# A modulation vector computed by rows on VectorE instead of by columns with TensorE sums, and in another stage of the first layer

## The chip, the cores and the metric

The kernel runs on one core of one Trainium2 chip. The metric is the device time of one execution in microseconds (us); lower is better. Several executions are timed, and their median counts.

## The reference

Two trunk layers work on 256 context tokens and 1024 latent tokens of width 1024. Each layer has a mixing part (four groups of recurrent heads: HGRN2, mLSTM, retention and GLA, each scanned forward and backward) and a channel part (a squared-ReLU MLP of width 4096). Ahead of each part the tokens are normalised, scaled and shifted, and behind it a gate scales what is added to the residual. These shifts, scales and gates are the modulation: for each layer a vector of 6 x 1024 numbers for the latent tokens and one for the context tokens.

```python
for layer in range(DEPTH):
    mod_l = (jax.nn.silu(c) @ w_ada[layer] + b_ada[layer])[:, None, :]
    mod_c = (jax.nn.silu(c_ctx) @ w_ada[layer] + b_ada[layer])[None, None, :]
    sh1_l, sc1_l, g1_l, sh2_l, sc2_l, g2_l = jnp.split(mod_l, 6, axis=-1)
    sh1_c, sc1_c, g1_c, sh2_c, sc2_c, g2_c = jnp.split(mod_c, 6, axis=-1)
    pl = split_proj(modulate(xl, sh1_l, sc1_l) @ w_in[layer])
    pc = split_proj(modulate(xc, sh1_c, sc1_c) @ w_in[layer])
    ...
    xl = xl + g1_l * mixer_out(raw_l, pl, g_heads[layer], w_out[layer])
    ...
    xl = xl + g2_l * sq_relu_mlp(modulate(xl, sh2_l, sc2_l), w_ff1[layer], w_ff2[layer])
```

The change is in how `silu(c) @ w_ada + b_ada` is computed, a product of one vector of 1024 with a 1024 x 6144 matrix, for two vectors and two layers.

## The kernel before

Tokens lie along the free dimension, channels on the 128 partitions. Each dense product is made of three matrix products of split operands (`mm3`, lines 293 to 295: high by high, high by low, low by high), so TensorE has most of the work.

The stages of a layer, in order: `mix_open` (normalisation and the first dense products), `mixers`, `outproj`, and `mlp`. In `mixers` the four recurrent groups run one after the other: GLA, HGRN2 (two halves), mLSTM (two halves), retention (two halves). Beside each, `Fill` advances a queue of dense products in small steps, to give TensorE work while the scan waits for VectorE and ScalarE. In the first layer's `mixers` three of five of these steps also advance a generator, `fill.also`, which computes two thirds of layer 0's modulation (r = 1 and 2; the third r = 0 is made at the start, by `ada_unit`). In the first layer's `mlp` the function `filler` advances another such generator behind each of 32 tiles; it computes all of layer 1's modulation. A framework then sets the final order on each engine from this program; the engines work in order, each through its own queue.

The generator is `ada_part`. For each strip of W columns of `w_ada` it loads eight blocks of 128 input rows (128 x W, through SyncE's queue, line 402), and for each token VectorE multiplies a block by the 128 scalars of the vector on the partitions and adds it to an accumulator (lines 406 and 408). Then TensorE sums the accumulator over the partitions by products with a column of ones (line 413), and VectorE adds the bias (line 419). In the first layer W is 256, with four buffers for blocks; in `mlp` W is 512, with four too.

Names: `ph`, `px`, `pw`, `po`, `pc` are SBUF pools of the stages, `st` the pool that stays (constants, temporaries, `mod`), `psum` the PSUM banks. `mod` holds the modulation, 48 columns for each layer and token.

Of the kernel before, what the change touches and what calls it, by code (L numbers as in the profile page):

```python
# [6 lines left out]
F32 = mybir.dt.float32  # L7
# [3 lines left out]
ALU = mybir.AluOpType  # L11
# [4 lines left out]
NK = 8  # L16
# [181 lines left out]
class K:  # L198
    def __init__(self, ctx, tc, io):
# [3 lines left out]
        dp = ctx.enter_context(tc.tile_pool(name="dp", bufs=1, space=bass.MemoryType.DRAM))  # L203
# [12 lines left out]
        self.d_a = dp.tile([2, 4, NC], F32, name="d_a")  # L216

# [98 lines left out]
    def params(self, tmp):  # L316
        nc = self.nc
        c2 = self.o["cc"](256)
        a, b = tmp.sub(0, 256)(256), tmp.sub(256, 256)(256)
        self.logsig(b, c2, a)  # L320
        nc.scalar.activation(b, b, AF.Exp)
        nc.vector.tensor_tensor(c2, c2, b, op=ALU.mult)

# [67 lines left out]
    def ada_part(self, l, r, toks, wring, tmp, acc, banks, W):  # L391


        nc = self.nc
        one = self.m64[:, 1:2]
        nt, nb = len(toks), W // 128
        for q in range(2048 // W):
            g, h = divmod(q * W, 512)
            A = [b(W) for b in acc[:nt]]
            for k in range(NK):  # L400
                w = wring.next()(W)
                nc.sync.dma_start(w, self.io["w_ada"][l, r, k, :, g, h:h + W])
                for i, j in enumerate(toks):
                    c = self.cc[:, k, j:j + 1]
                    if k == 0:
                        nc.vector.tensor_scalar(A[i], w, c, None, op0=ALU.mult)
                    else:
                        nc.vector.scalar_tensor_tensor(A[i], w, c, A[i], op0=ALU.mult, op1=ALU.add)
                yield
            ps = self.bank(banks().next())  # L410
            for i in range(nt):
                for cb in range(nb):
                    nc.tensor.matmul(ps[:, 2 * cb + i:2 * cb + i + 1], lhsT=A[i][:, 128 * cb:128 * cb + 128], rhs=one,  # L413
                                     start=True, stop=True)
            o = 16 * r + nb * q
            mo = self.mod[:, l, o:o + nb, toks[0]:toks[0] + nt]
            bb = self.bada[:, l, o:o + nb].unsqueeze(2).to_broadcast([128, nb, nt])
            v = ps[:, 0:2 * nb].rearrange("p (c j) -> p c j", j=2)[:, :, 0:nt]
            nc.vector.tensor_tensor(mo, v, bb, op=ALU.add)
            if (r == 0 and g >= 2) or (r == 2 and g < 2):  # L420
                nc.vector.tensor_scalar(mo, mo, 1.0, None, op0=ALU.add)
            yield
# [997 lines left out]
    def mixers(self, l, ada):  # L1420
        nc, hp = self.nc, self.heap

        fill = Fill(5)
# [32 lines left out]
        ao = hp.alloc(1536, True) if l == 0 else None  # L1456
        if l == 0:
            fill.also = ada([ao.sub(256 * i, 256) for i in range(6)], lambda: self.dbanks)
# [17 lines left out]
        self.rt_setup()  # L1476
        for p in range(2):
# [93 lines left out]
def build(ctx, tc, io):  # L1571
# [17 lines left out]
    for l in range(2):  # L1589
# [4 lines left out]
        def ada(bufs, banks):  # L1594
            for r in (1, 2):
                yield from b.ada_part(0, r, (0, 1), Ring(bufs[:4]), None, bufs[4:6], banks, 256)
# [8 lines left out]
        def ada1(bufs, l=l):  # L1605
            for r in range(3) if l == 0 else ():
                yield from b.ada_part(1, r, (0, 1) if r == 0 else (1,), Ring(bufs[:4]), None, bufs[4:6], lambda: b.banks, 512)
# [3 lines left out]
        def filler():  # L1611
            for _ in range(4):
                next(gen, None)
# [64 lines left out]
def host(x, c, ctx, c_ctx, w_ada, b_ada, w_in, g_heads, hgrn_lb_logits, ml_gate_bias, rt_decay_logit,  # L1678
# [29 lines left out]
    A["w_ada"] = ca(w_ada.reshape(2, 8, 128, 3, 4, 512).transpose(0, 3, 1, 2, 4, 5))  # L1708
# [29 lines left out]
```

## Time and profile before

| | us |
|---|---|
| median of 3 runs | 3308.24 |
| lowest, highest | 3303.61, 3309.18 |
| the profiled execution, its own time | 3300.05 |
| its span, first to last instruction | 3298.2 |
| TensorE busy | 3215.6 (97%) |
| VectorE busy | 2121.8 (64%) |
| ScalarE busy | 1286.1 (39%) |
| TensorE's granted clock, mean | 0.992 of full speed |

An engine's busy time says little where matrix products are pipelined; what ends last is read from the chain, the sequence of steps followed back from the last instruction, and from who waited for whom in a stretch. In the rows, PE is TensorE, PEld its weight load, DVE VectorE, ACT ScalarE, POOL GpSimd, and SP SyncE, whose queue (SPq) issues the transfers.

### The profile page before, as it was taken

Reading aid. Unit: us, or ns where it says so; the run is one execution under the profiler, and the core shown is the slowest. Engines: PE = TensorE matmul, PEld = TensorE weight load, DVE = VectorE, ACT = ScalarE, POOL = GpSimd, SP = SyncE. Lnnn points to the kernel's source line nnn. Section 1 sums busy time; section 2 is a strip of 40 time slices with the busy share of each in tenths; the row PEclk is TensorE's granted clock in tenths of the full one; section 3 lists DMA queues with packets and bytes.
Section 4 is the critical chain, followed back from the end, with each engine's and each line's share of the span. In section 5 each row is a group of like instructions: output and inputs, shape, how many; then the busy total and the mean of one; then the engine's idle time right before and its main releaser. Section 6 shows DMA issues by size and latency. Waiting matters only on the chain.

```text
span 3298.2 us, 52930 instructions
## 1 busy us (share of the span) xinstructions
PE 3215.6 (97%) x20936; PEld 2640.0 (80%) x20936; DVE 2121.8 (64%) x4218; ACT 1286.1 (39%) x2665; POOL 10.8 (0%) x41
## 2 busy tenths in 40 slices
PE   7998899999999999999999999999999999999998
PEld 4786688877888888888888678788778888888887
DVE  4778887787666656555655586866756555554546
ACT  4665565445322122121212565765445322222222
POOL 0000000000000000000000000000000000000000
PEclk9999899999999999999999999999999999999999
DMA  5113444434322222222211222333315111111111
GB/s 206 61 50 127 122 133 148 121 101 146 103 80 71 83 65 80 69 64 64 77 39 34 76 66 77 110 114 109 103 58 163 53 50 46 51 51 46 51 48 65
DMA packets 175010, 278.85 MB, mean 85 GB/s; under 512 B 21097, under 2 KB 66825, under 8 KB 174505
## 3 DMA queue, kind: packets, MB, share of 16 engines
q1 hardware_dynamic: 173464, 273.66, 26.5%
q8 instruction: 164, 2.69, 0.3%
q10 hardware_dynamic: 1296, 1.81, 0.2%
q14 instruction: 86, 0.70, 0.1%
HBM read 229.75 MB, written 45.64 MB: 83 GB/s over the span
## 4 chain that ended last, share of the span: by engine, by line
PE 88%; DVE 5%; DMA 3%; ACT 3%; issue 1%; SPq 0%; DVEq 0%; ACTq 0%
PE psum L293 23%; PE psum L294 23%; PE psum L295 23%; PE psum L830 2%; PE psum L600 2%; PE psum L631 2%; PE psum L633 2%; PE psum L632 1%; PE psum L817 1%; PE psum L833 1%; PE psum L1018 1%; PE psum L705 1%; PE psum L1357 1%; PE psum L413 1%; DVE px L990 1%
## 5 line engine op out<-in xcount | busy, mean ns | idle before, releaser
L525 DVE SCALAR_TENSOR_TENSOR x<-psum,st,x 128x512 f32<-128x512 f32 (+1 forms) x648 | 441.3, 690 | 213.2 <-PE psum L295 212.3
L281 ACT ACTIVATE pc<-st 128x512 fp32r<-128x512 f32 x256 | 161.2, 632 | 847.5 <-PE psum L294 808.7
L294 PE MATMUL psum<-pc,pc 128*128 128x512 f32 (+1 forms) x1296 | 475.9, 367 | 0.0
L293 PE MATMUL psum<-pc,pc 128*128 128x512 f32 (+1 forms) x1296 | 475.8, 367 | 0.0
L295 PE MATMUL psum<-pc,pc 128*128 128x512 f32 (+1 forms) x1296 | 473.8, 366 | 0.0
L293 PE MATMUL psum<-Hhi,pc 128*128 128x512 f32 (+1 forms) x1280 | 471.9, 369 | 1.7 <-ACT pc L281 1.5
L294 PE MATMUL psum<-Hlo,pc 128*128 128x512 f32 (+1 forms) x1280 | 471.9, 369 | 0.1
L295 PE MATMUL psum<-Hhi,pc 128*128 128x512 f32 (+1 forms) x1280 | 470.5, 368 | 0.0
L293 PE MATMUL psum<-Hhi,pw 128*128 128x512 f32 (+1 forms) x1192 | 451.0, 379 | 5.7 <-ACT pw L281 2.5
L295 PE MATMUL psum<-Hhi,pw 128*128 128x512 f32 (+1 forms) x1192 | 445.2, 374 | 0.0
L294 PE MATMUL psum<-Hlo,pw 128*128 128x512 f32 (+1 forms) x1192 | 444.8, 373 | 0.0
L504 DVE TENSOR_TENSOR st<-st 128x256 f32<-128x256 f32 (+1 forms) x160 | 101.8, 637 | 301.8 <-ACT pc L503 300.7
L293 PEld LDWEIGHTS psum<-pc,pc 128*128 128x128 f32 x1296 | 244.4, 189 | 43.8 <-DVE x L525 1.3
L295 PEld LDWEIGHTS psum<-pc,pc 128*128 128x128 f32 x1296 | 244.0, 188 | 43.0 <-issue 2.7
L294 PEld LDWEIGHTS psum<-pc,pc 128*128 128x128 f32 x1296 | 244.5, 189 | 41.3 <-issue 2.1
L293 PEld LDWEIGHTS psum<-Hhi,pc 128*128 128x128 f32 x1280 | 241.2, 189 | 43.5 <-ACT pc L281 2.4
L294 PEld LDWEIGHTS psum<-Hlo,pc 128*128 128x128 f32 x1280 | 241.3, 189 | 40.9 <-DVE Hlo L481 0.5
L295 PEld LDWEIGHTS psum<-Hhi,pc 128*128 128x128 f32 x1280 | 241.1, 188 | 40.9 <-DVE pc L282 0.6
L293 PEld LDWEIGHTS psum<-Hhi,pw 128*128 128x128 f32 x1192 | 226.7, 190 | 51.4 <-issue 10.1
L282 DVE TENSOR_TENSOR pc<-st,pc 128x512 fp32r<-128x512 f32 x256 | 175.5, 690 | 137.9 <-ACT pc L281 117.3
L295 PEld LDWEIGHTS psum<-Hhi,pw 128*128 128x128 f32 x1192 | 226.2, 190 | 37.6 <-issue 2.1
L294 PEld LDWEIGHTS psum<-Hlo,pw 128*128 128x128 f32 x1192 | 226.8, 190 | 36.2 <-issue 2.2
(398 smaller groups left out, 4950.4 us busy)
## 6 DMA issues: line engine op xcount, KB each, us to landing
st<-w_ff SPq DMA_DIRECT2D x256, 256.0 KB
st<-w_inT SPq DMA_DIRECT2D x96, 256.0 KB
ph<-w_ada SPq DMA_DIRECT2D x128, 128.0 KB
st<-w_out SPq DMA_DIRECT2D x50, 256.0 KB
pc<-w_ada SPq DMA_DIRECT2D x48, 256.0 KB
st<-w_ada SPq DMA_DIRECT2D x48, 256.0 KB
d_z<-st SPq DMA_DIRECT2D x40, 256.0 KB
ps<-w_ada SPq DMA_DIRECT2D x32, 256.0 KB
```

The costliest lines, as they stand in the source:

```text
L281: nc.scalar.activation(hi, raw, AF.Copy)
L282: (eng or nc.vector).tensor_tensor(lo, raw, F(hi), op=ALU.subtract)
L293: t.matmul(out, lhsT=w[0], rhs=m[0], start=first, stop=False)
L294: t.matmul(out, lhsT=w[0], rhs=m[1], start=False, stop=False)
L295: t.matmul(out, lhsT=w[1], rhs=m[0], start=False, stop=last)
L413: nc.tensor.matmul(ps[:, 2 * cb + i:2 * cb + i + 1], lhsT=A[i][:, 128 * cb:128 * cb + 128], rhs=one, start=True, stop=True)
L504: nc.vector.tensor_tensor(r, r, r, op=ALU.mult)
L525: nc.vector.scalar_tensor_tensor(x, ps, self.mod[:, l, 40 + o, j:j + 1], x, op0=ALU.mult, op1=ALU.add)
L600: t.matmul(ps[:, 0:304], lhsT=h[a], rhs=u[b], start=(k + i == 0), stop=(k == NK - 1 and i == 2))
L631: t.matmul(ps[:, e, :], lhsT=h[0], rhs=u[0], start=(k == 0), stop=False)
L633: t.matmul(ps[:, e, :], lhsT=h[1], rhs=u[0], start=False, stop=(k == NK - 1))
L830: nc.tensor.matmul(o, lhsT=ST[r0:r0 + kd, c, d, :], rhs=qd[d](c)[r0:r0 + kd, :], start=(j == 0), stop=False, tile_position=(r0, 0))
```

## The change

`ada_part` is replaced by `ada_rows`. The weights are stored transposed, so that an output column lies on a partition and the 1024 inputs along the row. For each token and each half of 512 inputs, the vector is loaded once, copied to all 128 partitions (from `d_c` in DRAM, to which GpSimd's queue writes it at the start). Then for each of 16 blocks of 128 outputs, 512 weights for each output are loaded, and one VectorE instruction multiplies them by the copied vector and writes the sum along the row to a scratch column in the other layer's part of `mod`. TensorE has no part in it. The weights are loaded once for each token, not once for both.

In the first layer the generator starts later: not ahead of HGRN2, but ahead of mLSTM. It has two buffers of 128 x 512 for weights and one for the vector, in place of four of 128 x 256 and two accumulators, and its transfers are issued from GpSimd's queue. In `mlp` there are four buffers for weights and two for the vector, on SyncE's queue, and `filler` takes three steps instead of four.

```diff
+            nc.gpsimd.dma_start(self.d_c[j].rearrange("(k p) -> p k", p=128), self.cc[:, :, j])
...
-    def ada_part(self, l, r, toks, wring, tmp, acc, banks, W):
...
-            for k in range(NK):
-                w = wring.next()(W)
-                nc.sync.dma_start(w, self.io["w_ada"][l, r, k, :, g, h:h + W])
-                for i, j in enumerate(toks):
-                    c = self.cc[:, k, j:j + 1]
-                    if k == 0:
-                        nc.vector.tensor_scalar(A[i], w, c, None, op0=ALU.mult)
-                    else:
-                        nc.vector.scalar_tensor_tensor(A[i], w, c, A[i], op0=ALU.mult, op1=ALU.add)
-                yield
-            ps = self.bank(banks().next())
-            for i in range(nt):
-                for cb in range(nb):
-                    nc.tensor.matmul(ps[:, 2 * cb + i:2 * cb + i + 1], lhsT=A[i][:, 128 * cb:128 * cb + 128], rhs=one,
-                                     start=True, stop=True)
...
+    def ada_rows(self, l, r, toks, wring, cs, queue):
...
+        S = self.mod[:, 1 - l, 0:16, :]
+        for j in toks:
+            for h in range(2):
+                c = cs.next()(512)
+                queue.dma_start(c, self.d_c[j:j + 1, 512 * h:512 * h + 512].to_broadcast([128, 512]))
+                for o in range(16):
+                    w = wring.next()(512)
+                    queue.dma_start(w, self.io["w_adaT"][l, r, o, :, 512 * h:512 * h + 512])
+                    nc.vector.scalar_tensor_tensor(w, w, 1.0, c, op0=ALU.mult, op1=ALU.mult,
+                                                   accum_out=S[:, o:o + 1, h])
+                    if o % 2:
+                        yield
+            mo = self.mod[:, l, 16 * r:16 * r + 16, j]
+            nc.vector.tensor_tensor(mo, S[:, :, 0], S[:, :, 1], op=ALU.add)
+            nc.vector.tensor_tensor(mo, mo, self.bada[:, l, 16 * r:16 * r + 16], op=ALU.add)
...
-            fill.also = ada([ao.sub(256 * i, 256) for i in range(6)], lambda: self.dbanks)
...
+        ao = hp.alloc(1536, True) if l == 0 else None
+        if l == 0:
+            fill.also = ada([ao.sub(512 * i, 512) for i in range(3)])
...
-                yield from b.ada_part(0, r, (0, 1), Ring(bufs[:4]), None, bufs[4:6], banks, 256)
+                yield from b.ada_rows(0, r, (0, 1), Ring(bufs[:2]), Ring(bufs[2:]), nc.gpsimd)
...
-                yield from b.ada_part(1, r, (0, 1) if r == 0 else (1,), Ring(bufs[:4]), None, bufs[4:6], lambda: b.banks, 512)
+                yield from b.ada_rows(1, r, (0, 1) if r == 0 else (1,), Ring(bufs[:4]), Ring(bufs[4:]), nc.sync)
...
-            for _ in range(4):
+            for _ in range(3):
```

Three places show what moves. The first is VectorE's queue in the first layer, at the start of mLSTM's first half (`px` and `ph` hold the scan's operands). Before, the modulation has no instruction in this piece:

```order
L1338 TENSOR_TENSOR px_0_688<-px_0_688,psum 128x384
L1351 TENSOR_TENSOR px_0_688<-psum,st 128x390 x2
L1338 TENSOR_TENSOR px_0_688<-px_0_688,psum 128x384
L1360 TENSOR_TENSOR px_0_688<-px_0_688,psum 128x390
L1334 TENSOR_TENSOR ph_0_251<-ph_0_251,st 128x384
L1334 TENSOR_TENSOR px_0_688<-px_0_688,st 128x384
L1360 TENSOR_TENSOR px_0_688<-px_0_688,psum 128x390
```

With the change, the same scan instructions (their lines are six lower) have pairs of the row product (line 406) between them:

```order
L406 SCALAR_TENSOR_TENSOR ph_0_254,st<-ph_0_254 128x512 x2
L1332 TENSOR_TENSOR px_0_691<-px_0_691,psum 128x384 x3
L1345 TENSOR_TENSOR px_0_691<-psum,st 128x390 x2
L1354 TENSOR_TENSOR px_0_691<-px_0_691,psum 128x390 x2
L406 SCALAR_TENSOR_TENSOR ph_0_254,st<-ph_0_254 128x512
L1360 TENSOR_TENSOR px_0_691<-px_0_691,st 128x12
L406 SCALAR_TENSOR_TENSOR ph_0_254,st<-ph_0_254 128x512
L1361 RECIPROCAL px_0_691<-px_0_691 128x12
```

So two row products stand behind every few scan instructions, 128 in all from the head of mLSTM to the last gates of `mixers`; the 160 products of the old form ahead of mLSTM are gone from VectorE's queue.

The second is GpSimd's queue, which held no transfer before. From the head of mLSTM it holds (`MEMSET` of `px` are the scan's state columns):

```order
L402 DMA ph_0_254<-d_c 128x512
L1283 MEMSET px_0_691 128x65
L405 DMA ph_0_254<-w_adaT 128x512 x2
L1284 MEMSET px_0_691 128x65
L405 DMA ph_0_254<-w_adaT 128x512 x15
L402 DMA ph_0_254<-d_c 128x512
L405 DMA ph_0_254<-w_adaT 128x512 x10
```

All 128 loads of weights and 8 of the vector stand there, one behind the other; each waits for the row product that last read its buffer, two products back.

The third is VectorE's queue in the first layer's `mlp`, at its second tile (line 498 squares an activation, line 499 makes its low part, line 283 the low part of a weight tile):

```order
L406 SCALAR_TENSOR_TENSOR pc_4_8587,st<-pc_4_8587,st 128x512
L406 SCALAR_TENSOR_TENSOR pc_5_8588,st<-pc_5_8588,st 128x512
L498 TENSOR_TENSOR st<-st 128x256
L406 SCALAR_TENSOR_TENSOR st<-st 128x512
L499 TENSOR_TENSOR pc_9_8592<-st,pc_8_8591 128x256
L406 SCALAR_TENSOR_TENSOR st<-st 128x512
L498 TENSOR_TENSOR st<-st 128x512
L406 SCALAR_TENSOR_TENSOR pc_4_8587,st<-pc_4_8587,st 128x512
L499 TENSOR_TENSOR pc_9_8592<-st,pc_8_8591 128x512
L406 SCALAR_TENSOR_TENSOR pc_5_8588,st<-pc_5_8588,st 128x512
L406 SCALAR_TENSOR_TENSOR st<-st 128x512 x2
L283 TENSOR_TENSOR pc_0_8583<-st,pc_0_8583 128x512
```

Here the 128 products of the second layer stand from the second to the 20th of the 96 low parts (line 499) of the stage. The 128 of the old form stood from ahead of the first to behind the 76th.

## Rows read from the trace of the kernel before

**Rows 1.** The page: busy time (share of the span) and number of instructions.

```profile
PE 3215.6 (97%) x20936; PEld 2640.0 (80%) x20936; DVE 2121.8 (64%) x4218; ACT 1286.1 (39%) x2665; POOL 10.8 (0%) x41
```

**Rows 2.** The page: the chain that ended last, by engine.

```profile
PE 88%; DVE 5%; DMA 3%; ACT 3%; issue 1%; SPq 0%; DVEq 0%; ACTq 0%
```

**Rows 3.** Windows: length, busy us of each engine (instructions), clock, DMA share, GB/s.

```profile
200.00:553.00 353.00, 324.98 (x3418) 264.75 (x3398) 290.12 (x734) 204.68 (x465) 1.28 (x12) 0.96 0.38 118
553.00:817.00 264.00, 260.81 (x1809) 211.95 (x1807) 200.89 (x508) 126.55 (x320) 0.24 (x2) 1.00 0.40 119
...
952.00:1120.00 168.00, 168.00 (x887) 144.78 (x885) 110.95 (x181) 34.62 (x62) 0.00 (x0) 1.00 0.25 74
```

**Rows 4.** Windows of line 413 alone: PE, PEld busy us.

```profile
200.00:553.00 353.00, 10.43 (x72) 10.60 (x72) 0.96 0.38 118
553.00:817.00 264.00, 6.95 (x56) 7.33 (x56) 1.00 0.40 119
```

**Rows 5.** The chain from 937 to 1810 us, by line.

```profile
by line: PE psum L293 32.6%; PE psum L294 32.5%; PE psum L295 32.3%; PE psum L413 1.5%; DMA pc<-w_ada 0.5%; DVE st L476 0.5%; DVE Hlo L481 0.3%; DVE st L408 0.2%; DVE st L406 0.0%; issue 0.0%; DVEq L408 0.0%
```

**Rows 6.** Windows of line 408 alone: DVE busy us.

```profile
200.00:553.00 353.00, 62.57 (x140) 0.96 0.38 118
553.00:817.00 264.00, 37.18 (x84) 1.00 0.40 119
952.00:1120.00 168.00, 28.20 (x40) 1.00 0.25 74
```

**Rows 7.** Waits of PE, 200 to 553 us: total, times, longest.

```profile
PE psum L1018 <- DVE px L990: 10.3, 6, 4.6
PE psum L833 <- ACT px L1043: 6.2, 5, 3.0
PE psum L413 <- DVE ph L408: 3.5, 1, 3.5
```

**Rows 8.** Waits of PE, 553 to 817 us: all there are.

```profile
PE psum L1343 <- DVE px L802: 0.8, 1, 0.8
PE psum L1329 <- DVE px L1351: 0.6, 1, 0.6
```

**Rows 9.** Line 408: duration ns min/median/max, first and last start, form.

```profile
L408 DVE SCALAR_TENSOR_TENSOR ph<-ph,st x224: 413/479/491, 281.0 to 749.6; 128x256 f32<-128x256 f32 x112
L408 DVE SCALAR_TENSOR_TENSOR st<-st x64: 742/747/753, 952.9 to 1634.1; 128x512 f32<-128x512 f32 x64
```

**Rows 10.** VectorE's timeline: start us, us, instruction [idle before].

```profile
552.15 1.28 DVE L1303 TENSOR_TENSOR px<-psum,st 128x192 f32<-128x192 f32 x4 [1.75 <-PE psum L830]
...
952.92 2.07 DVE L408 SCALAR_TENSOR_TENSOR st<-st 128x512 f32<-128x512 f32 x3
...
817.38 0.68 DVE L650 TENSOR_TENSOR st<-st,psum 128x512 f32<-128x512 f32 x1
...
1116.06 0.69 DVE L505 TENSOR_TENSOR pc<-st,pc 128x512 fp32r<-128x512 f32 x1
```

**Rows 11.** The chain's transfers: start us, us from issue to landing, transfer.

```profile
577.73 4.32 DMA ph<-d_u
791.73 3.81 DMA st<-d_yg
796.46 3.42 DMA st<-w_out
803.48 4.64 DMA st<-w_out
...
1928.01 2.32 DMA ph<-d_a
```

**Rows 12.** Line 402, SyncE's queue: ns to issue one, min/median/max.

```profile
L402 SPq DMA_DIRECT2D ph<-w_ada x128: 327/332/1240, 223.7 to 743.6; - x128
```

More of the change, by code (lines that the diff above doesn't have):

```diff
@@ L216, in __init__ @@
         self.d_a = dp.tile([2, 4, NC], F32, name="d_a")
+        self.d_c = dp.tile([2, 1024], F32, name="d_c")
     @staticmethod
@@ L322, in params @@
         nc.vector.tensor_tensor(c2, c2, b, op=ALU.mult)
+        for j in range(2):
+            nc.gpsimd.dma_start(self.d_c[j].rearrange("(k p) -> p k", p=128), self.cc[:, :, j])
     def params2(self, tmp):
@@ L389, in ada_finish @@
             nc.vector.tensor_scalar(m, m, 1.0, None, op0=ALU.add)
-    def ada_part(self, l, r, toks, wring, tmp, acc, banks, W):
+    def ada_rows(self, l, r, toks, wring, cs, queue):
         nc = self.nc
[L395 to L399, printed above, removed]
-            for k in range(NK):
-                w = wring.next()(W)
-                nc.sync.dma_start(w, self.io["w_ada"][l, r, k, :, g, h:h + W])
-                for i, j in enumerate(toks):
-                    c = self.cc[:, k, j:j + 1]
-                    if k == 0:
-                        nc.vector.tensor_scalar(A[i], w, c, None, op0=ALU.mult)
-                    else:
-                        nc.vector.scalar_tensor_tensor(A[i], w, c, A[i], op0=ALU.mult, op1=ALU.add)
-                yield
-            ps = self.bank(banks().next())
-            for i in range(nt):
-                for cb in range(nb):
-                    nc.tensor.matmul(ps[:, 2 * cb + i:2 * cb + i + 1], lhsT=A[i][:, 128 * cb:128 * cb + 128], rhs=one,
-                                     start=True, stop=True)
[L415 to L420, printed above, removed]
@@ new lines, in ada_rows @@
+        S = self.mod[:, 1 - l, 0:16, :]
[13 more added lines that the diff above has]
+            nc.vector.tensor_tensor(mo, mo, self.bada[:, l, 16 * r:16 * r + 16], op=ALU.add)
+            if r in (0, 2):
+                mo = self.mod[:, l, 16 * r + (8 if r == 0 else 0):16 * r + (16 if r == 0 else 8), j]
@@ L1454, in mixers @@
         fill.until(m)
-        ao = hp.alloc(1536, True) if l == 0 else None
-        if l == 0:
-            fill.also = ada([ao.sub(256 * i, 256) for i in range(6)], lambda: self.dbanks)
         self.feat_hg(hg[0])
@@ L1592, in build, with ada @@
         b.mix_open(l)
-        def ada(bufs, banks):
+        def ada(bufs):
             for r in (1, 2):
-                yield from b.ada_part(0, r, (0, 1), Ring(bufs[:4]), None, bufs[4:6], banks, 256)
+                yield from b.ada_rows(0, r, (0, 1), Ring(bufs[:2]), Ring(bufs[2:]), nc.gpsimd)
         b.mixers(l, ada)
@@ L1707, in host @@
     A["gla_w"] = ga
-    A["w_ada"] = ca(w_ada.reshape(2, 8, 128, 3, 4, 512).transpose(0, 3, 1, 2, 4, 5))
+    A["w_ada"] = ca(w_ada[:1, :, :2048].reshape(1, 8, 128, 1, 4, 512).transpose(0, 3, 1, 2, 4, 5))
+    A["w_adaT"] = ca(w_ada.transpose(0, 2, 1).reshape(2, 3, 16, 128, 1024))
     at = _cols()
```

## The prediction

> **What bounds the kernel now.** I read the page first: TensorE is busy 97% of the span and VectorE 64% [rows 1], and the chain that ended last is TensorE's for 88% [rows 2]. So a matrix product that goes away gives time back, if nothing else comes to hold TensorE up. An average over the span hides where VectorE is close, so I then cut the span at the places that the change touches [rows 3]. From 200 to 553 us (the end of GLA and HGRN2) VectorE is busy 290 of 353 us, and TensorE stands still for 28 us. From 553 to 817 us (mLSTM, retention, last gates) VectorE has 201 of 264 us and TensorE 261. From 952 to 1120 us, early in the MLP, TensorE is busy without a gap. The waits tell who holds whom: in HGRN2 TensorE waits 10.3 us for VectorE's line 990 and 3.5 us for the modulation itself [rows 7], in mLSTM and retention only 1.4 us in all [rows 8]. The reader is to see that the change takes work from a stretch where VectorE is late and puts it into one where TensorE is never kept waiting, but where VectorE has 63 us free at most.
>
> **What is removed.** The sums over partitions on TensorE (line 413) are busy 10.4 us from 200 to 553 and 7.0 us from 553 to 817 [rows 4]; where groups overlap with their neighbours a little less comes back, so I take 7.5 and 6. In the MLP the chain shows them with 1.5% of 873 us, 13.1 us [rows 5]. VectorE loses 62.6 us of line 408 before 553 [rows 6]. TensorE's waits there for VectorE and for line 408 sum to 13.8 us [rows 7]; those on line 990 have causes of their own too, so I take 5 us (bounds 0 and 13.8). Gains, if all that is added were hidden: 7.5 + 5 + 6 + 13.1 = 31.6 us.
>
> **What is added to mLSTM and retention.** 128 row products stand between the first instruction of mLSTM (line 1303, at 552 us) and the last gates (line 650, at 817 us) [rows 10], 64 pairs in 264 us, 4.1 us for a pair. A row product with a sum as second output isn't in the trace. The nearest row is line 408 at the same size, with two SBUF inputs: 0.75 us, or 0.69 us each in a run of three [rows 9, 10]. I take 0.75, as low bound 0.69, as high bound twice as much. VectorE's other work in the stretch is 200.9 - 37.2 (line 408) - some 5 (lines 406, 419), that is 159 us; with 128 x 0.69 = 88 it is 247 of 264 us. By load alone it fits, barely.
>
> By latency it doesn't. There are two buffers. A load can be issued only when the product two back has read its buffer, and VectorE, which works in order, stands at the next product until the load has landed; everything of the scan and of the gates that is queued behind it stands too, and TensorE waits for that (lines 1329 to 1360, and PSUM banks that VectorE empties). So a pair can't come faster than one landing and one product. No transfer from GpSimd's queue is in the trace of before. The nearest rows are SyncE's transfers: 2.3 us for one of 2.5 KB, 3.4 to 4.6 us for 256 KB and 4.3 us for the 192 KB of `d_u` [rows 11], with 0.33 us of issue included [rows 12]. Low bound 3.0 (between a tiny one and the shortest of 256 KB), high bound 5 (the longest of these rows, and one issue more). I take 3.8, the shortest rows being from a queue of the same kind of transfer and the stretch having moderate traffic (DMA share 0.40 [rows 3], to which 136 transfers of 256 KB in place of 48 of 128 KB come, 29 MB more). Then a pair costs 3.8 + 0.75 = 4.55 us, and 64 pairs 291 us. Eight times the vector is loaded ahead of the weights in the same queue, behind the last product of 16; an issue and part of a transfer each, 6 us in all. The pairs aren't evenly spread, and where a stretch between two is longer than 4.55 us for another reason, that comes on top; 10 us (bounds 0 and 40). Sum 307 against 264 now: **+43 us**, in which the 6 us of line 413 are no longer a gain, since TensorE isn't the bound there any more.
>
> **What is added to the MLP.** The 128 products stand up to the 20th low part (line 505 before, at 1116 us [rows 10]), within 168 us. VectorE's other work there is 111.0 - 28.2 - 2 = 81 us [rows 3, 6]; with 128 x 0.69 = 88 it has 169 of 168 us. There are four buffers, so latency takes 32 rounds of 4.55 us, 146 us: not the limit on average, but products stand in runs. TensorE has eight banks to write ahead, which cover some us, and behind 1120 us VectorE has much less to do than now. I take a loss of 8 us (bounds 0 and 40). SyncE's queue holds weight loads behind loads that wait for VectorE; the weight buffers hold half a stage of two tiles, so I cost that at nothing; if that cover is gone it belongs to the same 40.
>
> **At no cost:** the two writes of `d_c` at the start (nobody reads them for 500 us), the few additions for the bias, and the loads themselves (the DMA engines are 0.25 to 0.40 busy [rows 3]).
>
> **Sum:** -7.5 - 5 + 43 - 13.1 + 8 = +25 us. Made against the profiled execution that is 3300 + 25 = 3325; the median of the runs shown is 8 us above that execution, so the forecast for a median is 3308 + 25 = **3333 us**.
>
> **Where the Trainium skill speaks against the change.** The rows show a product with two f32 inputs in SBUF at 0.75 us for 512 columns and 0.48 for 256 [rows 9], hence 0.27 us for 256 columns more. "Vector Engine (DVE) Microarchitecture Reference", section "Points that are easy to get wrong", says that this form with two SBUF sources that aren't bf16 runs at half throughput, since no read port is left for the accumulator. The rows of line 408 agree only in part: without a second output no halving is seen. "SBUF — State Buffer", section "SBUF: two separate sides", says that for a transfer issued from GpSimd the descriptors are written by GpSimd's cores, which VectorE's two-port operations lock out of SBUF meanwhile; no run so far shows it. The two are rivals below, priced from rows.
>
> **Rivals.**
> - *The ring keeps up (faster).* If a landing takes 3.2 us or less, a pair takes less than the 4.1 us there are; or TensorE has enough other work to ride over the stalls. For it: TensorE waits 1.4 us for VectorE there now [rows 8], so there is slack. Against: VectorE would be 94% busy. Gains 31.6, less some 5: 3281 us. It decides below 4.1 us for a pair.
> - *Break-even:* a pair costs about 4.2 us. Around 3308.
> - *The product is slower with a sum:* by the columns, 2 x 0.27 us more, 1.28 us. A pair is then 3.8 + 1.28 = 5.1 us, the stretch 325 + 16, +77 us. In the MLP VectorE has 81 + 128 x 1.2 = 235 us in 168, of which TensorE's slack covers some 10: +55. With 25.6 of gains: 3308 + 106 = 3414 us.
> - *GpSimd's transfers land late*, 4.64 us [rows 11] or more, because VectorE or its own queue holds them: 5.4 us a pair, 345 + 16 us, +97; 3308 - 25.6 + 97 + 8 = 3388 us.
>
> **Chances.** The forecast 0.45 (own range 3315 to 3360), the ring keeps up 0.25, break-even 0.10, slow product 0.09, late landing 0.11. The range for 8 in 10 leaves out the lower part of "keeps up" and most of the slow product: 3279 to 3395. A difference of 0.2% (6.6 us) is about what a measurement of this kernel can tell from none. Faster by more: 0.25; within: 0.10; slower: 0.65.
>
> **What will show it.** Right: VectorE's waits for transfers `ph<-w_adaT` and `ph<-d_c` sum to several ten us from 553 on; the stretch from the first line 1297 to the last gate is near 307 us; TensorE waits there for VectorE; the MLP has no line 413, and VectorE is full for its first 170 us; HGRN2 ends some 12 us earlier. Wrong: a row product that differs from 0.75 us; a landing of 3 us or of 5 and more; TensorE still without gaps in mLSTM while VectorE waits; weight loads of the MLP so late that TensorE waits for them.

## The result and the profile after

The changed kernel takes 3343.84 us (median of 4 runs, 3337.05 to 3349.44), the kernel before, measured beside it, 3307.5: 1.0111 times as long, interval 1.0089 to 1.0132, some 36 us. The forecast was 3333, slower by 25. The profiled execution took 3337.05 us, its span is 3335.3. Two executions among all that follow ran far longer (6461 us with the vector written late, 15371 us with the rows spread) and count in no ratio; the trace of the late write is of the first, whose granted clock falls to 0.16 from 2637 us on, so that only its first layer is read. The page of the changed kernel, busy times and the chain by engine, which answer to [rows 1, 2]:

```profile
PE 3213.7 (96%) x20680; PEld 2629.7 (79%) x20680; DVE 2105.7 (63%) x4331; ACT 1283.5 (38%) x2665; POOL 85.9 (3%) x179
...
PE 75%; issue 7%; DVE 7%; DMA 5%; ACT 3%; POOL 2%; SPq 1%; POOLq 0%; DVEq 0%; ACTq 0%
```

TensorE has 256 products fewer and is busy about as long; the span is 37 us longer. The page doesn't say where, so I cut both traces at the same instructions: the first and last start of the HGRN2-type scan step (line 990 before, 984 after; GLA and HGRN2 lie between), the last sum of the first layer's output projection (line 1564, 1558), and the last of its MLP (line 525, 519).

| stretch | before, us | after, us | difference | forecast |
|---|---|---|---|---|
| start, to the first scan step | 120.3 | 128.2 | +7.9 | 0 |
| GLA and HGRN2, first to last step | 423.2 | 394.5 | -28.7 | -12.5 |
| mLSTM, retention, last gates, output projection | 389.9 | 451.6 | +61.7 | +43 |
| MLP of the first layer | 913.8 | 908.4 | -5.4 | -5 |
| the second layer, to its last MLP sum | 1439.1 | 1440.4 | +1.3 | 0 |
| sum | | | +36.8 | +25.5 |

The sum came out near the forecast because two large terms were too small on opposite sides. Part of that comes from the boundary between the two stretches: 87 dense products (`denseV`, lines 631 to 633 before) run behind the last scan step in the kernel before and ahead of it in the changed one, so the same work leaves one stretch and enters the other. That doesn't touch the net of the two, +33.0 us, where the forecast had +30.5. Windows of the second and third stretch, of before:

```profile
core 0: us, PE busy (x) PEld busy (x) DVE busy (x) ACT busy (x) POOL busy (x), PEclk, DMA share, GB/s
120.30:543.50 423.20, 393.60 (x4208) 319.76 (x4207) 345.52 (x850) 253.31 (x568) 1.28 (x12) 0.96 0.34 107
543.50:933.40 389.90, 382.62 (x2475) 315.64 (x2473) 273.53 (x639) 173.38 (x405) 0.24 (x2) 1.00 0.38 116
```

and of the changed kernel, with the early MLP, which answers to the last of [rows 3]:

```profile
128.20:522.70 394.50, 386.82 (x4223) 315.55 (x4222) 293.00 (x690) 253.68 (x579) 1.77 (x12) 1.00 0.28 91
522.70:974.30 451.60, 397.88 (x2332) 322.61 (x2330) 313.15 (x788) 170.70 (x395) 72.88 (x138) 0.91 0.52 163
...
993.00:1171.00 178.00, 171.66 (x879) 146.55 (x878) 159.31 (x400) 36.42 (x65) 0.00 (x0) 0.98 0.72 229
```

Read length minus PE's busy time, which is TensorE's idle time: 29.6 us before and 7.7 after in GLA and HGRN2; 7.3 and 53.7 in the stretch behind. There TensorE is also busy 15 us longer with 143 products fewer (56 sums and those 87), at a granted clock of 0.91 instead of 1.00. So the loss has two parts, idle time and products that run at the lower of the clock's two levels. Shorter windows show the two together:

```profile
600.00:620.00 20.00, 19.31 (x146) 14.20 (x144) 14.45 (x54) 9.97 (x28) 4.35 (x9) 1.00 0.69 213
620.00:640.00 20.00, 14.84 (x81) 13.07 (x81) 14.41 (x48) 3.57 (x11) 4.24 (x8) 0.58 0.53 168
...
840.00:860.00 20.00, 2.72 (x11) 2.00 (x10) 12.71 (x29) 8.90 (x16) 2.15 (x4) 0.62 0.69 232
```

The row product and the load, by their lines (duration ns min/median/max, first and last start):

```profile
L406 DVE SCALAR_TENSOR_TENSOR ph<-ph x128: 674/692/695, 532.6 to 854.4; 128x512 f32<-128x512 f32 x128
L406 DVE DVE_READ_ACCUMULATOR ph<-ph x128: 77/83/85, 533.2 to 855.0; 128x1 f32 x128
```

```profile
L405 POOL DMA_DIRECT2D ph<-w_adaT x128: 537/537/554, 527.6 to 850.9; - x128
...
DMA to landing us min/median/max: 2.7/3.4/7.0
```

The product costs 0.69 us and a second instruction, which fetches the sum, 0.08: 0.77 in all, as forecast (0.75). The 128 products take from 532.6 to 855.0 us, 5.04 us for a pair (forecast 4.55 and the unevenness). VectorE waits for the loads, as forecast, and GpSimd for the products; the waits from 527 to 861 us:

```profile
DVE ph L406 <- DMA ph<-w_adaT: 62.6, 64, 4.6
DVE ph L406 <- DMA ph<-d_c: 9.6, 6, 3.0
...
POOL ph L405 <- DVE ph L406: 173.5, 72, 7.3
```

TensorE's waits there are short and spread over many lines, but for one, at the output projection's first weights (line 294 for line 282):

```profile
PE psum L294 <- ACT po L282: 16.8, 1, 16.8
PE psum L811 <- DVE ph L1128: 5.9, 2, 3.9
PE psum L1337 <- DVE px L796: 5.6, 2, 3.8
```

The chain shows what that one waits for (start us, us, what):

```profile
850.87 3.53 DMA ph<-w_adaT
854.42 0.71 DVE ph L406 x2
855.15 0.63 ACT po L282
855.78 0.52 ACT st L309
856.30 1.05 ACT po L282 x2
857.35 1.28 DVE po L283 x2
```

The weights of `po` are written where the pool `ph` was, and `ph` holds the ring of the modulation: the last row product releases the next stage.

### The profile page after: what moved, and what is told of

The parts are those of the page before. It is cut to its first block, busy times and chain, and to the rows that moved or that the text cites. A ratio compares the mean times of both kernels' runs of the same rounds, so it can differ in the third digit from the quotient of the medians.

```text
span 3335.3 us, 52597 instructions
## 1 busy us (share of the span) xinstructions
PE 3213.7 (96%) x20680; PEld 2629.7 (79%) x20680; DVE 2105.7 (63%) x4331; ACT 1283.5 (38%) x2665; POOL 85.9 (3%) x179
## 4 chain that ended last, share of the span: by engine, by line
PE 75%; issue 7%; DVE 7%; DMA 5%; ACT 3%; POOL 2%; SPq 1%; POOLq 0%; DVEq 0%; ACTq 0%
PE psum L294 20%; PE psum L295 20%; PE psum L296 20%; PE psum L594 2%; POOL ph L405 2%; PE psum L824 1%; PE psum L625 1%; DMA ph<-w_adaT 1%; PE psum L627 1%; PE psum L626 1%; PE psum L1012 1%; PE psum L827 1%; DMA ps<-w_ada 1%; PE psum L811 1%; DVE px L984 1%
```

## The experiments

The theory of the prediction, **latency**: two buffers make a round of a landing and a product, and VectorE stands meanwhile. The rival, **load**: VectorE's time for the products, taken in order from between the scan's instructions, is the price, loads or no loads. A third, that came with the trace, **place or form**: whether the row form costs, or any work of VectorE at this place. In the table the stretch is from the last HGRN2 step to the last sum of the output projection, in each kernel's trace; for the shared loads the execution in the trace took 3344.3 us, 10 above their median.

| kernel | median us | ratio to before (interval) | HGRN2 us | stretch us | TensorE idle | PE busy, clock | DVE busy |
|---|---|---|---|---|---|---|---|
| before | 3307.5 | | 423.2 | 389.9 | 7.3 | 382.6, 1.00 | 273.5 |
| changed | 3343.8 | 1.0111 (1.0089 to 1.0132) | 394.5 | 451.6 | 53.7 | 397.9, 0.91 | 313.2 |
| no generator | 3261.5 | 0.9864 (0.9846 to 0.9882) | 391.9 | 371.7 | 3.4 | 368.3, 1.00 | 234.7 |
| products, few loads | 3327.1 | 1.0056 (1.0041 to 1.0071) | 395.1 | 432.6 | 37.7 | 394.9, 0.92 | 310.3 |
| ring of four | 3345.7 | 1.0115 (1.0095 to 1.0136) | 392.9 | 454.2 | 52.6 | 401.6, 0.91 | 313.7 |
| shared loads | 3334.1 | 1.0077 (1.0058 to 1.0097) | 392.9 | 445.8 | 40.3 | 405.5, 0.89 | 312.9 |
| SyncE's queue | 3313.4 | 1.0012 (1.0000 to 1.0024) | 395.0 | 425.4 | 37.8 | 387.6, 0.93 | 312.5 |
| old form moved, paced | 3342.9 | 1.0103 (1.0085 to 1.0121) | 393.1 | 456.9 | 39.2 | 417.7, 0.91 | 329.3 |
| rows spread from HGRN2 | 3298.5 | 0.9970 (0.9958 to 0.9983) | 430.5 | 378.0 | 11.0 | 367.1, 0.97 | 250.0 |

In this table all kernels with row products, but the last, have 2332 or 2334 products of TensorE in the stretch, and no generator 2340. The kernel before has 2475 there and the moved old form 2477, with 56 and 128 sums among them; the last kernel has 2261.

**What the work costs at all.** The generator of the first layer is left out.

```diff
+        nc.gpsimd.memset(self.o["mod"](192), 0.0)
...
-        ao = hp.alloc(1536, True) if l == 0 else None
-        if l == 0:
-            fill.also = ada([ao.sub(512 * i, 512) for i in range(3)])
...
```

> The change without the first layer's generator: r = 1 and 2 of the first layer's modulation are left out (zeros), with their loads and products; the MLP's part and the write of the vector at the start remain. It shows what the work costs at all. From mLSTM's first step to the last gates it should take 250 to 262 us (272.9 before, less 7.0 us of sums and the waits), the time 3344 - 72 to 3344 - 84, 3260 to 3272. If it stays above 3290, the loss isn't from the products and loads but from the other order of the scan and the dense work.

3261.47 us, as foretold. The stretch's window, beside that of the changed kernel above:

```profile
521.50:893.20 371.70, 368.28 (x2340) 303.08 (x2338) 234.74 (x525) 172.77 (x407) 0.31 (x2) 1.00 0.33 106
```

Without the work, TensorE is idle for 3.4 us at a mean clock of 1.00. With it nearly the same number of products takes 79.9 us longer: 50.3 us idle and 29.6 us of slower products. VectorE is busy 78.4 us more, though it looks to be idle for a third of the stretch. That the two are alike is no rule: with SyncE's queue, below, the same VectorE time goes with 53.7 us. In the kernel before, 38.8 us of the old form's VectorE work stood here (273.5 less 234.7), and the stretch was 18.2 us longer than without; but 14.3 of these are TensorE's time for 135 products more (382.6 less 368.3), and only 3.9 are idle time (7.3 less 3.4).

**Latency, taken away in two ways.** Four weight buffers instead of two (`carve` takes them from another part of the heap, where there is room):

```diff
-        ao = hp.alloc(1536, True) if l == 0 else None
+        ao = carve(hp, 1, "lo", 2560) if l == 0 else None
...
-                yield from b.ada_rows(0, r, (0, 1), Ring(bufs[:2]), Ring(bufs[2:]), nc.gpsimd)
+                yield from b.ada_rows(0, r, (0, 1), Ring(bufs[:4]), Ring(bufs[4:]), nc.gpsimd)
```

> The change with four weight buffers of 128 x 512 in the first layer instead of two (one for the vector, as in the change); the same loads, the same products, GpSimd's queue. Latency theory (a pair can't come faster than one landing and one product, and VectorE waits 62.6 us for these loads): four loads in flight, 3.4 + 4 x 0.77 = 6.5 us for four, 104 us in 32 rounds where 64 pairs took 322; VectorE's waits for w_adaT fall below 15 us, the stretch from mLSTM to the last gates goes from 334 to 270 to 285 us, the time is 3285 to 3300. Load theory (VectorE with 128 x 0.77 = 99 us more in 264 is what holds the stretch, and 34 MB of transfers): the waits move elsewhere, the stretch stays above 315, the time is 3325 to 3344.

And the products without most loads:

```diff
-                    queue.dma_start(w, self.io["w_adaT"][l, r, o, :, 512 * h:512 * h + 512])
+                    if l == 1 or o < 2:
+                        queue.dma_start(w, self.io["w_adaT"][l, r, o, :, 512 * h:512 * h + 512])
```

> The change with the 128 row products of the first layer, but only 16 of its 128 weight loads are issued (two for each token and half; the other products read the buffers as they stand, so the first layer's r = 1 and 2 of the modulation are wrong numbers). Latency theory: VectorE doesn't wait for loads, the stretch from mLSTM to the last gates is 265 to 280 us, the time 3280 to 3295. Load theory (VectorE's own 99 us): above 315 us, 3325 to 3344. Compared with the ring of four: if both are as fast, neither the traffic nor GpSimd's issues cost anything; if only this one is fast, they do.

The ring of four took 3345.72 us, no less than the ring of two. The products of that kernel, and VectorE's waits in the stretch:

```profile
L417 DVE SCALAR_TENSOR_TENSOR px<-px x128: 626/686/694, 529.2 to 778.3; 128x512 f32<-128x512 f32 x128
```

```profile
DVE px L417 <- DMA px<-w_adaT: 18.2, 18, 2.7
...
DVE px L417 <- DMA px<-d_c: 8.2, 5, 2.9
```

The latency theory foretold shorter waits (below 15 us for the weights; 18.2 came, and 26.4 with the vector's, instead of 72.2) and with them an earlier end of the products (778 instead of 855 us), and was wrong about what they are worth. The wait for the next stage's weights isn't in this trace either, as these buffers lie elsewhere, and the stretch is no shorter (454.2). With few loads, 3327.05 us: 17 us less than the change, and still 61 us (432.6 less 371.7) more than no generator in the stretch. In that kernel the products stand closer: 39 of the 128 start between 600 and 640 us (16 in the changed kernel), and there TensorE falls behind (window of that kernel from 580 us on):

```profile
580.00:640.00 60.00, 42.04 (x206) 33.42 (x207) 47.03 (x156) 14.99 (x41) 5.07 (x11) 0.60 0.33 106
```

So in this kernel most of the loss needs no load. That speaks for the load theory, with two reservations. The framework orders each engine's queue anew for each kernel, so the products also stand at other places of the scan, and a wait less can be paid for by a worse place. And how close the products stand is a rival of its own: no run spaces them evenly without the loads. The kernel with all its loads on SyncE's queue, below, has a shorter stretch (425.4 us), so the 61 us aren't the least that VectorE's work costs here.

**Half the loads.** Each block is loaded once and multiplied for both tokens.

```diff
...
+            for o in range(16):
+                w = wring.next()(512)
+                queue.dma_start(w, self.io["w_adaT"][l, r, o, :, 512 * h:512 * h + 512])
+                for j, out in ((0, junk(512)), (1, w)):
+                    nc.vector.scalar_tensor_tensor(out, w, 1.0, c[j], op0=ALU.mult, op1=ALU.mult,
+                                                   accum_out=S[:, j, o:o + 1, h])
+                yield
...
```

> Each weight block of the first layer is loaded once and multiplied for both tokens (two weight buffers, two for the vectors, one for the first product's unused output): 64 loads instead of 128, the same 128 products. Latency theory: two loads and four products in a round, 3.4 + 4 x 0.77 = 6.5 us, 32 rounds, 208 us, below the 264 that there are: the stretch is 275 to 295 us, the time 3287 to 3310, a little behind the ring of four. Load theory: 3325 to 3344.

3334.13 us, inside the load theory's forecast: 10 us less than the change with half the transfers, and 74 us above no generator in the stretch. The traffic isn't what costs most.

**The queue.**

```diff
-                yield from b.ada_rows(0, r, (0, 1), Ring(bufs[:2]), Ring(bufs[2:]), nc.gpsimd)
+                yield from b.ada_rows(0, r, (0, 1), Ring(bufs[:2]), Ring(bufs[2:]), nc.sync)
```

> The change with the first layer's transfers issued from SyncE's queue instead of GpSimd's. Theory one (GpSimd's issue of 0.54 us and its landing are what make a round long): 0.2 us less for each issue, 0.2 to 0.5 us a pair, 13 to 30 us less, 3314 to 3330. Theory two (a load that waits for VectorE holds up the loads of dense weights and scan rows queued behind it on SyncE): TensorE waits for those, the stretch grows, 3350 to 3400.

3313.4 us, 30 less than the change: theory one, a little more than it foretold. The issues of SyncE's queue in the first layer, and VectorE's waits for these loads:

```profile
L405 SPq DMA_DIRECT2D ph<-w_adaT x128: 327/328/1170, 533.9 to 823.5; - x128
```

```profile
DVE ph L406 <- DMA ph<-w_adaT: 26.1, 40, 2.2
...
DVE ph L406 <- DMA ph<-d_c: 3.9, 6, 1.1
```

An issue is 0.33 us instead of 0.54. And GpSimd begins it later. Two rows of the changed kernel's VectorE and one of its GpSimd show it (start us, us):

```profile
650.61 0.69 DVE L406 SCALAR_TENSOR_TENSOR ph<-ph 128x512 f32<-128x512 f32 x1 [0.76 <-DMA ph<-w_adaT]
651.23 0.08 DVE L406 DVE_READ_ACCUMULATOR ph<-ph 128x1 f32 x1
```

```profile
651.61 0.54 POOL L405 DMA_DIRECT2D ph<-w_adaT  x1 [1.40 <-DVE ph L406]
```

The product ends at 651.30 and its buffer's next load is issued at 651.61; over the 126 such pairs of the trace the median gap is 0.30 us, with SyncE's queue 0.03. From the first product's start to the last one's end it is 322.5 us on GpSimd's queue and 289.4 on SyncE's, 5.04 and 4.52 us a pair: 0.52 us a pair, 33 us in all, where the medians differ by 30. The later start is 0.27 us of it. The longer issue would be another 0.21, if a landing is later by all of it; that isn't shown, since the 3.4 us of a landing are counted from the start of the issue, and the trace has no landings for SyncE's loads. So with two buffers a shorter round ends the stretch earlier, as the latency theory has it. The same reservation stands, as VectorE's order also differs between the two kernels, and the waits alone don't decide: VectorE waits 30.0 us for these loads here and 26.4 in the ring of four, which takes 32 us longer. There up to 15 products start within 20 us, here no more than 10. GpSimd's queue also holds MEMSETs of the scan behind the loads, but in the changed kernel's trace no engine waits for one from 120 to 975 us. Theory two isn't seen: SyncE's queue has room, though the loads wait in it.

**Place or form.** The old form everywhere, its start moved ahead of mLSTM:

```diff
-        ao = hp.alloc(1536, True) if l == 0 else None
-        if l == 0:
-            fill.also = ada([ao.sub(256 * i, 256) for i in range(6)], lambda: self.dbanks)
         self.feat_hg(hg[0])
...
+        ao = hp.alloc(1536, True) if l == 0 else None
+        if l == 0:
+            fill.also = ada([ao.sub(256 * i, 256) for i in range(6)], lambda: self.dbanks)
         for p in range(2):
             self.fetch(ml[p], "K", MLK + p, TBS)
```

> The old form everywhere (column products, TensorE sums, four buffers of 128 x 256, SyncE's queue); only the place moves: the first layer's generator starts ahead of mLSTM, not ahead of HGRN2. Theory one (what HGRN2 gains comes from taking VectorE's work away, as the waits say: 27 us of TensorE's waits before, 7 after, and the sums): the stage of GLA and HGRN2 goes from 432 to about 399 us here too. Theory two (only the sums on TensorE and the waits named in the prediction come back): to about 419. For mLSTM and retention, load says VectorE has 201 + some 85 of 264 us, so the stage grows by 10 to 40 us; the time is then 3285 to 3330. If the row form with its two buffers is what costs and not the place, this kernel is faster than before; if the place costs, it is as slow as the change.

3369.53 us (ratio 1.0191, 1.0176 to 1.0205), slower than foretold. The reason is in the pace: the 145 dense steps from there on give the generator 87 steps, and it has 144. The other 57 ran at the end with nothing beside them; the window from 842 us on:

```profile
842.00:893.00 51.00, 16.52 (x77) 15.79 (x78) 40.45 (x105) 4.08 (x7) 0.00 (x0) 0.51 0.39 127
```

So it was mended with a step at every dense step:

```diff
-                if self.also and self.n % 5 in (0, 2, 4):
+                if self.also:
```

> The old form at the new place again (ahead of mLSTM), but with a step of the generator at every step of the dense work, 145 for its 144; at three of five 57 steps were left and ran at the end with nothing beside them (51 us at a clock of 0.51). Theory one (VectorE's time inside the scan of mLSTM and retention is the price, in either form): the stretch from HGRN2's end to the end of the output projection costs as much as with row products from SyncE's queue or somewhat more, 425 to 445 us, and the time is 3308 to 3330. Theory two (the old form with four buffers does no harm there, so it is the row form that costs): 390 to 400 us, with HGRN2's gain of 25 to 33 us kept, 3275 to 3295.

3342.93 us, above the range of theory one and far from theory two: the old form at the new place costs as much as the change. HGRN2 gains 30 us here too (393.1 against 423.2), the stretch loses 67. The window:

```profile
513.30:970.20 456.90, 417.68 (x2477) 343.56 (x2476) 329.33 (x798) 170.98 (x395) 0.39 (x3) 0.91 0.38 120
```

For the old form it is the place that costs, with the closer steps that go with it: 34 us against the kernel before. For the row form the price of the place alone isn't shown. With SyncE's queue and the vector written late (both below) it takes 3306.4 us at the new place, as long as the kernel before; started ahead of HGRN2 at another pace it takes 3298.5. Between the old form here and the row form with both changes lie 36.6 us, which the row form in the change loses again: 30.4 by GpSimd's queue and 7.0 by the write at the start.

**The parts apart.** Row products in the first layer only, and in the MLP only; the other part has the old form.

```diff
-                yield from b.ada_rows(1, r, (0, 1) if r == 0 else (1,), Ring(bufs[:4]), Ring(bufs[4:]), nc.sync)
+                yield from b.ada_part(1, r, (0, 1) if r == 0 else (1,), Ring(bufs[:4]), None, bufs[4:6], lambda: b.banks, 512)
...
-            for _ in range(3):
+            for _ in range(4):
```

> Row products in the first layer's mLSTM and retention as in the change; in the MLP the old form (column products and TensorE sums). By the stages of the profiles the MLP gave 5 us and the first layer cost 41, so 3308 + 41 = 3349 us, 5 above the changed kernel. Rival: the MLP's part is worth nothing or costs, then 3344 or less. By the prediction's terms (13.1 us of sums back, 8 lost) also 3349.

```diff
-                yield from b.ada_rows(0, r, (0, 1), Ring(bufs[:2]), Ring(bufs[2:]), nc.gpsimd)
+                yield from b.ada_part(0, r, (0, 1), Ring(bufs[:4]), None, bufs[4:6], banks, 256)
```

> Row products in the MLP only; in the first layer the old form at its old place, ahead of HGRN2. The vector is still written at the start. Theory one: +8 us at the start, -5 in the MLP: 3311 us. If the write at the start costs nothing in the end: 3303. If the row products in the MLP hold TensorE up as much as the sums did: 3316.

The first layer alone: 3338.03 us, 1.0102 (1.0085 to 1.0119); the MLP alone: 3312.34 us, 1.0016 (1.0006 to 1.0025). Foretold were 3349 and 3311. The first layer's part is the whole loss. In the traces the MLP takes 913.4 us with the old form and 908.6 with rows, 913.8 and 908.4 in the two kernels of the change: 5 us less each time; in the other kernels with rows there it is 907.4 to 912.8, so 1 to 6 us less. By the medians the rival's forecast came true (3344 or less), as the first layer alone is no slower than the change; but an interval of theirs is 11 us wide and can't settle five. In the MLP-only kernel HGRN2 took 12 us longer than before (435.0) with the same 4208 products and the same idle time of TensorE (29.7 us), which was busy 11.7 us longer at a granted clock of 0.93 instead of 0.96. Why the clock was lower stays open.

**The start.** The vector is written later, in HGRN2; first by its place in the program:

```diff
-        for j in range(2):
-            nc.gpsimd.dma_start(self.d_c[j].rearrange("(k p) -> p k", p=128), self.cc[:, :, j])
...
+        if l == 0:
+            for j in range(2):
+                nc.gpsimd.dma_start(self.d_c[j].rearrange("(k p) -> p k", p=128), self.cc[:, :, j])
         self.feat_hg(hg[0])
```

> The change whole, but the vector is written to DRAM from the middle of the first layer's recurrent groups, not at the start. Theory one (the 2 x 1024 elements of 4 bytes hold up the first weight loads, which landed after 9.4 to 13.8 us instead of 5.3): the first HGRN2-type scan step starts near 120 us again instead of 128, and the time is 3344 - 8 = 3336 us. Theory two (the start is late for the order of its loads, or the lateness is absorbed later): no change, 3340 to 3347.

3339.98 us and 128.4 us to the first scan step, as in the change. It tells nothing: GpSimd's queue was empty, and the write was issued at 14.8 us again. It amounts to a second measurement of the change (1.0099, 1.0084 to 1.0114). So the vector was copied to a temporary first, in the kernel with SyncE's queue:

```diff
...
+        if l == 0:
+            a = self.tD.next()(2, NK)
+            nc.vector.tensor_copy(a, self.cc[:, :, 0:2].rearrange("p k j -> p j k"))
+            for j in range(2):
+                nc.gpsimd.dma_start(self.d_c[j].rearrange("(k p) -> p k", p=128), a[:, j, :])
...
```

> The change with the first layer's loads from SyncE's queue, and the vector written to DRAM only in HGRN2 (through a copy in a temporary that is in use until then, since without it the write was issued at 15 us again). Theory one (the 4-byte elements hold up the first weight loads): the first HGRN2-type scan step starts near 120 us, not 127.4, and the time is 3313 - 7 = 3306 us. Theory two (the late start has another cause in the order of the first loads): 127 us and 3313.

3306.37 us (0.9998, 0.9987 to 1.0010), and 120.2 us to the first scan step: what theory one foretold, to the microsecond. In its trace GLA and HGRN2 take 396.3 us and the stretch behind them 426.5, as with SyncE's queue alone (395.0, 425.4), so it is the start that gives the 7 us. The first 30 us of the changed kernel, and of this one:

```profile
0.00:30.00 30.00, 10.37 (x36) 2.69 (x38) 6.22 (x42) 4.92 (x16) 2.15 (x6) 0.93 0.92 245
```

```profile
0.00:30.00 30.00, 16.21 (x72) 4.51 (x72) 6.06 (x42) 7.64 (x23) 0.20 (x4) 1.00 0.94 327
```

The DMA engines are as busy (0.92, 0.94) and move a quarter less while the 8 KB of the vector are written, and the first weights come late (the chain of the changed kernel, start us, us; the longest landing in the first 30 us of the chain before is 5.9):

```profile
15.91 12.34 DMA ps<-w_ada
```

The program writes elements of 4 bytes; the trace records 32 packets of 256 bytes, from 17 to 24 us. That the small elements are the cause isn't shown, since no run writes the same bytes at this time in larger pieces. Shown is what the write costs where it stands.

**A version that is faster than both.** With SyncE's queue and the late write the generator starts ahead of HGRN2 again, and one in three of the dense steps advances it.

```diff
-                if self.also and self.n % 5 in (0, 2, 4):
+                if self.also and self.n % 3 == 0:
...
+        ao = hp.alloc(1536, True) if l == 0 else None
+        if l == 0:
+            fill.also = ada([ao.sub(512 * i, 512) for i in range(3)])
         self.feat_hg(hg[0])
...
```

> As the run before, and the generator starts ahead of HGRN2, as in the kernel before the change, with a step at every third step of the dense work instead of three of five, so that its 68 steps are spread over 250 steps instead of the first 113 of 145. Two weight buffers, SyncE's queue, the same products. If the loss is VectorE's time taken from the scan of mLSTM and retention in a dense run, spreading it gives the sums on TensorE back (17 us) without the stretch's loss: HGRN2 ends 5 to 20 us later than in the change, mLSTM to the last gates takes 270 to 280 us, and the time is 3280 to 3297. If it is each round's wait for a landing that costs, wherever it stands, HGRN2 loses what mLSTM gains: 3303 to 3315.

3298.54 us, 0.9970 (0.9958 to 0.9983): 9 us faster than before, 45 faster than the change, and a microsecond or two above the better theory's range. The row products aren't spread over both stretches: they run from 233 to 698 us, 100 of the 128 ahead of the boundary. HGRN2 pays (430.5 us, more than foretold; TensorE is idle 28.1 us there), and the stretch behind it is at 378.0 us, 6 above no generator, with 28 row products and with 79 products of TensorE less, which run earlier. Place and pace change together here, so what each is worth isn't shown.

```profile
123.20:553.70 430.50, 402.38 (x4284) 326.98 (x4282) 349.38 (x895) 255.01 (x574) 1.29 (x12) 0.98 0.45 147
553.70:931.70 378.00, 367.05 (x2261) 299.18 (x2259) 249.96 (x585) 171.08 (x400) 0.24 (x2) 0.97 0.38 122
```

## Why the prediction was right, and where it wasn't

**-7.5 and -5, HGRN2.** Measured -28.7. TensorE is 6.8 us less busy, near the 7.5 of the sums, but that is luck: 72 sums went (10.4 us), the 87 dense products came in, and the granted clock was 1.00 instead of 0.96. The relief was mis-sized: TensorE's idle time fell by 21.9 us, not 5. I had counted two of the three waits of [rows 7] and discounted them from 13.8 to 5. In this stretch the two go from 14.5 us to 3.4, and the third, 5.8 us for ScalarE, which I had left out, goes to 0.2; the rest are short ones. TensorE's waits in the changed kernel, 128.2 to 522.7 us:

```profile
PE psum L1012 <- DVE px L984: 3.4, 10, 0.5
...
PE psum L827 <- ACT px L1037: 0.2, 1, 0.2
```

VectorE has 52.5 us less work there. The old form moved shows the same (393.1 us), so the gain doesn't need the row form. In the last kernel, with row products and without sums in HGRN2, TensorE is idle for 28.1 us again, which speaks for VectorE's time and against the sums as the cause.

**+43, mLSTM and retention.** Measured +61.7, the term that was mis-sized most. Its working was the ring: 4.55 us a pair, measured 5.04, with 0.77 for the product (right), 3.4 for the landing (3.8 foretold) and 0.30 of GpSimd's start (not foretold). These three make 4.47, so the ring by itself was sized well, by errors that cancel. The 0.57 us left over, 36 us in 64 pairs, stand against 16 for the vector's loads and the uneven spread; that is the term of the sum that was too small, though within its bounds. The direction and the waits were as the text had them. But the mechanism was only part of it. "By load alone it fits, barely" is the sentence that fell: with few loads the products still cost 61 us over no generator, and four buffers gave nothing back. VectorE's free 63 us were in part gaps in which it waited for ScalarE and TensorE within the scan. Its two longest waits in the kernel before, 553 to 817 us:

```profile
DVE st L708 <- ACT st L707: 15.9, 8, 5.9
DVE px L1360 <- PE psum L1357: 7.7, 8, 2.4
```

That work in such gaps holds up the scan is a reading that fits the runs, but it isn't shown apart from the closeness of the products and the new order. Three things had no term: the lower clock (29.6 us against no generator), the next stage's weights behind the ring's last product (16.8 us), and that a shorter wait is given back when the products then stand closer. How the 80 us divide between the ring and the load can't be told, as the order changes with each kernel: the few-loads kernel would put 61 on the load, but with SyncE's queue the ring and the load together are 53.7.

**-13.1 and +8, MLP.** Measured -5.4, foretold -5, by two errors that cancel: TensorE is 10.7 us less busy (13.1 foretold) and 5.3 us more idle (8 foretold). The whole MLP of the first layer, before and after:

```profile
933.40:1847.20 913.80, 909.55 (x4764) 776.24 (x4764) 545.24 (x898) 210.12 (x374) 1.82 (x4) 1.00 0.23 68
```

```profile
974.30:1882.70 908.40, 898.84 (x4639) 764.05 (x4639) 542.37 (x1022) 210.16 (x374) 1.86 (x4) 1.00 0.25 80
```

Early in it VectorE was nearly as full as worked out: 159.3 of 178 us, where TensorE was idle 6.3. The runs apart don't contradict it and don't prove it.

**At no cost: the writes of the vector.** Wrong, 7 us, shown by the late write.

**The rivals.** The ring didn't keep up. The product isn't slow: "Vector Engine (DVE) Microarchitecture Reference" of the Trainium skill, section "Points that are easy to get wrong", would have the form at half throughput, and the trace has 0.692 us and 0.083 for the sum, against 0.75 for the same size without a sum [rows 9], and 0.75 too with one source in PSUM (line 1564 before); here the measurement decides against it. Late landings weren't it either, with a median of 3.4 us. "SBUF — State Buffer" of the Trainium skill, section "SBUF: two separate sides", has GpSimd's descriptors held up by VectorE's two-port operations; the row shows landings by the median no later than those of [rows 11], the longest 7.0 us, and whether VectorE's operations here are of that kind no row tells. What GpSimd's queue did cost lay ahead of the transfer, in its start and perhaps its issue.

## What to carry to other kernels

Don't take the free time of an engine inside a scan for room: with 39 us of VectorE's time there TensorE was idle 4 us more, with 78 us it was idle 34 to 50 us more, at a lower clock besides. Price the place and the form of a moved piece apart, by moving the old form: here it cost as much as the change. Then look at the queue that issues the transfers: here it was worth 30 of the 36 us. When a piece ends late, look at whose memory it holds, since the next stage may be laid over it (16.8 us of TensorE's waiting here).

## What the hardware showed that I had not expected

Two writes of 4 KB, element by element, landed after 10.2 and 12.1 us, and with them the core's transfers went at 245 GB/s over the first 30 us instead of 327. GpSimd starts a load 0.30 us after the product that frees its buffer and needs 0.54 us to issue it, SyncE's queue 0.03 and 0.33. A product with a sum is two instructions, 0.69 and 0.08 us. And the granted clock of the changed kernel was 0.58 of full speed from 620 to 640 us, where TensorE was busy for 14.8 of the 20 us, and 0.62 from 840 to 860, where it was busy for 2.7, so that it had 1.2 instead of 2.4 GHz for most of these windows; in the kernel without a generator one 20 us window of the stretch was below 1.00, at 0.91.
